# Score matmuls of the first key tile placed ahead of the sums of the second one in a stick-breaking attention

## The chip, the core and the metric

The kernel runs on one core of a Trainium2 chip. The metric is device time in microseconds (us) of one execution; the median of three runs of the kernel before is 2151.57 us (2151.13 to 2152.0). Engines are named as in the profile: PE is TensorE's matmul and PEld its weight load, DVE is VectorE, ACT is ScalarE, POOL is GpSimd, SP is SyncE, which issues DMAs.

## What is computed

Two layers over 528 tokens (16 meta tokens and 512 frames) of width 1024. Each layer is a half SwiGLU, a mixer and a half SwiGLU. The mixer projects the normed input, runs a stick-breaking attention beside a convolution branch, gates and adds both and projects again. The attention is the part that matters here:

```python
def block(args):                       # for one block of queries, 8 heads of 64
    qb, start = args
    z = jnp.einsum('bhqd,bhkd->bhqk', qb, kh) * scale
    qpos = start + jnp.arange(Q_BLOCK, dtype=jnp.int32)[:, None]
    valid = key_pos < qpos
    log_keep = jnp.where(valid, jax.nn.log_sigmoid(-z), 0.0)
    after = lax.cumsum(log_keep, axis=3, reverse=True) - log_keep
    attn = jnp.where(valid, jnp.exp(jax.nn.log_sigmoid(z) + after), 0.0)
    return jnp.einsum('bhqk,bhkd->bhqd', attn, vh)
```

So the weight of a key needs the sums over all later keys up to the query. Key tiles are therefore worked from the last one (3) down to the first one (0).

## The kernel before

Everything is kept transposed: channels on the 128 partitions, tokens along the row. Each float32 matrix is split in a high and a low float32r part (`split`, L79 and L80: a cast on ACT, a subtraction on DVE), and each product is three matmuls (high·high, high·low, low·high). The weights of a projection come by DMA in units of 1024x128, are split by ACT (L224, L225) with a DMA that adds on POOL's queue (L226), and are prepared three units ahead (`LOOK`).

In the mixer, `attend(i, ...)` (called four times a layer, each time for a pair of heads) and `products()` (the projections q, k, v, gs and gc) are two generators that take turns. After each `yield` of `attend`, `next(beside)` issues one piece of a projection: 24 matmuls of 264 columns, or 12 of 512, at L720, into a PSUM tile `ps`, which DVE reads out at L795. The projections have nothing to do with the attention of the same pair; they are there to keep PE busy while ACT and DVE work on the scores. PE's order is exactly the order of the calls (`manual_schedule` at L987). On ACT, DVE, POOL and SP the scheduler sets the order.

For one pair, `attend` works in these steps. The opening transposes v (L836, L840) and multiplies the corner pieces (L845) into a PSUM tile `zt`. `scores(t)` multiplies q by k for key tile t (L877, six matmuls) and adds the mask (L880) into a PSUM tile `z`; then `softplus` goes over it: the absolute value (L814), Exp and Ln (L103) on ACT, a maximum and an addition on DVE (L817); then the split in `sh` and `sl`. `sums_and_weights(t)` adds the running sums onto the same `z` by matmuls with a matrix of ones and a triangle (L900, L902, L903), lets POOL fold `sl` into the next tile's (L906), and takes Exp of `z` on ACT (L913, recorded as L103, output `a`), which is split in `ah` and `al`. `values(t)` multiplies them by v (L921). The last three steps of a pair, `sums_and_weights(0)`, `values(1)` and `values(0)`, are run by `step` inside the next pair's `attend`, or after the last pair between the remaining projections.

The score tiles are five a pair, and the pool that holds them has two buffers, used in turn:

```python
tc.tile_pool(name=f"psz{l}", bufs=2, space=bass.MemoryType.PSUM, reuse_waits="tile") as psz:
...
    return psz.tile([P, 2, 512], F32, tag="z", name="z")
```

In the order zt, t=3, t=2, t=1, t=0 the tile of t=0 takes the buffer of t=2, and the next pair's `zt` takes the buffer of t=1. A tile's buffer is free for the next when all that read it are done; the last reader of a score tile is the Exp at L913.

The rest of this section prints the code with the profile's line numbers.

Of the kernel before, what the change touches and what calls it, by code (L numbers as in the profile page):

```python
# [60 lines left out]
def kernel(ctx, tc, hT, par, const, wg1, wu1, wd1, win, wao, wco, wout, wg2, wu2, wd2, out):  # L61
# [12 lines left out]
    def f(ap):  # L74
        return ap.bitcast(F32)

    def split(x, hi, lo):

        act.copy(hi, x)  # L79
        dve.tensor_tensor(out=lo, in0=x, in1=f(hi), op=ALU.subtract)  # L80
# [15 lines left out]
    def fn(out, in_, func, **kw):  # L96
        need = SETS[func]
        if table["set"] != need:
            load = act.preload_act_table_set(need)
            for p in table["acts"]:  # L100
                tc.add_manual_dep(load.ins, p.ins.name, NOSYNC, reason="table order")
            table.update(set=need, load=load, acts=[])
        i = act.activation(out, in_, func, **kw)  # L103
        tc.add_manual_dep(i.ins, table["load"].ins.name, NOSYNC, reason="table order")
        table["acts"].append(i)
# [570 lines left out]
    PIECES = ((3, 272, 256, 0), (2, 256, 272, 112), (1, 128, 400, 112), (0, 16, 512, 128))  # L676

    def mixer(l, st, omode, after):
        last = omode == XO
        with ExitStack() as es:  # L680
# [72 lines left out]
            with tc.tile_pool(name=f"psm{l}", bufs=2, space=bass.MemoryType.PSUM, reuse_waits="tile") as psp, \  # L753
                    tc.tile_pool(name=f"psz{l}", bufs=2, space=bass.MemoryType.PSUM, reuse_waits="tile") as psz:

                def ztile():
                    return psz.tile([P, 2, 512], F32, tag="z", name="z")
# [28 lines left out]
                with tc.tile_pool(name=f"att{l}", bufs=1, reuse_waits="tile") as ap_:  # L786
# [26 lines left out]
                    def softplus(dst, z, np_):  # L813
                        act.activation(dst, z, AF.Abs)  # L814
                        fn(dst, dst, AF.Exp, bias=bias[:np_, 3:4], scale=-1.0)
                        fn(dst, dst, AF.Ln, bias=bias[:np_, 2:3], scale=1.0)
                        dve.scalar_tensor_tensor(out=dst, in0=z, scalar=0.0, in1=dst, op0=ALU.max, op1=ALU.add)  # L817
# [6 lines left out]
                    def attend(i, step, qf, kf, vf):  # L824
# [45 lines left out]
                        def scores(t, q0, n, m0):  # L870
                            z = ztile()
                            ks = slice(t * P, (t + 1) * P)

                            for pi, (kk, qq) in enumerate(((kh, qh), (kh, ql), (kl, qh))):
                                for hh in range(2):
                                    r = slice(64 * hh, 64 * hh + 64)
                                    pe.matmul(z[:, hh, :n], kk[r, ks], qq[r, q0:q0 + n], start=(pi == 0), stop=False,  # L877
                                              skip_group_check=True)
                            for hh in range(2):
                                pe.matmul(z[:, hh, DEAD[t]:240 - m0], identb, maskb[:, m0 + DEAD[t]:], start=False, stop=False,  # L880
                                          skip_group_check=True)
                            d = DEAD[t]
                            sp = ap_.tile([P, 2, 512], F32, tag="big", bufs=BIG, name="sp")[:, :, d:n]
                            sh, sl = rests if t == 3 else (ap_.tile([P, 2, n], F32R, tag=f"s{x}{t}" if t else "big",
                                                                    bufs=1 if t else BIG, name=f"s{x}") for x in "hl")
                            softplus(sp, z[:, :, d:n], P)
                            if t == 3:
                                dve.tensor_tensor(out=sp[96:128, :, n - d - 16:], in0=sp[96:128, :, n - d - 16:],
                                                  in1=corner[96:128], op=ALU.subtract)
                            split(sp, sh[:, :, d:], sl[:, :, d:])  # L890
                            later[t] = (z, sh, sl, q0, n)

                        def sums_and_weights(t):
                            z, sh, sl, q0, n = later[t]
                            for hh in range(2):

                                for e in range(3, t, -1):
                                    _, ph, pl, pq, pn = later[e]
                                    for s in (ph, pl) if e == t + 1 else (ph,):
                                        pe.matmul(z[:, hh, pq - q0:pq - q0 + pn], onesm, s[:, hh, :], start=False,  # L900
                                                  stop=False, skip_group_check=True)
                                pe.matmul(z[:, hh, :n], trir, sh[:, hh, :], start=False, stop=False, skip_group_check=True)  # L902
                                pe.matmul(z[:, hh, :n], trir, sl[:, hh, :], start=False, stop=True, skip_group_check=True)  # L903
                            if 0 < t < 3:
                                _, _, pl, pq, _ = later[t + 1]
                                pool.tensor_tensor(out=sl[:, :, pq - q0:], in0=f(sl[:, :, pq - q0:]), in1=f(pl), op=ALU.add)  # L906
                            d = DEAD[t]
                            a = ap_.tile([P, 2, 512], F32, tag="big", bufs=BIG, name="a")[:, :, d:n]
                            ah, al = (ap_.tile([P, 2, 512], F32R, tag="big", bufs=BIG, name=nm)[:, :, :n]
                                      for nm in ("ah", "al"))  # L910
                            for p in (ah, al) if d else ():
                                pool.memset(f(p[:, :, :d]), 0.0)
                            fn(a, z[:, :, d:n], AF.Exp, bias=B_ZERO)  # L913
                            split(a, ah[:, :, d:], al[:, :, d:])
                            acts[t] = (ah, al, q0, n)
# [35 lines left out]
                        values(3)  # L951
                        sums_and_weights(2)
                        yield
                        sums_and_weights(1)
                        scores(*PIECES[3])
                        yield
                        values(2)
                        yield
# [28 lines left out]
                    with tc.manual_schedule(engines={mybir.EngineType.PE}):  # L987
                        for i in range(4):
                            for _ in attend(i, step, *parts(i)):
                                next(beside, None)  # L990
                        for n, fill in enumerate(FILL_END):
                            for _ in range(fill):
                                next(beside, None)
                            step(n)
                        for _ in beside:
                            pass
# [152 lines left out]
```

## Time and profile before

| What | us |
|---|---|
| median of three runs | 2151.57 |
| time of the profiled execution | 2152.29 |
| its span, first to last instruction | 2150.5 |
| PE busy in the span | 2135.9 (99%) |
| PEld busy | 2052.8 (95%) |
| DVE busy | 1521.5 (71%) |
| ACT busy | 1137.9 (53%) |
| POOL busy | 488.7 (23%) |

The granted clock of TensorE is 0.999 of full speed over the span. Busy shares are averages over the whole program; matmuls are pipelined, so their rows overlap, and what a matmul takes is read from the distance between the starts of two that follow each other. The attention of layer 0 lies at about 436 to 617 us, that of layer 1 at about 1512 to 1686 us. A boundary between two pairs is the opening (L836) of the next pair; there are three a layer.

### The profile page before, as it was taken

Reading aid. Unit: us, or ns where it says so; the run is one execution under the profiler, and the core shown is the slowest. Engines: PE = TensorE matmul, PEld = TensorE weight load, DVE = VectorE, ACT = ScalarE, POOL = GpSimd, SP = SyncE. Lnnn points to the kernel's source line nnn. Section 1 sums busy time; section 2 is a strip of 40 time slices with the busy share of each in tenths; the row PEclk is TensorE's granted clock in tenths of the full one; section 3 lists DMA queues with packets and bytes.
Section 4 is the critical chain, followed back from the end, with each engine's and each line's share of the span. In section 5 each row is a group of like instructions: output and inputs, shape, how many; then the busy total and the mean of one; then the engine's idle time right before and its main releaser. Section 6 shows DMA issues by size and latency. Waiting matters only on the chain.

```text
span 2150.5 us, 39932 instructions
## 1 busy us (share of the span) xinstructions
PE 2135.9 (99%) x16226; PEld 2052.8 (95%) x16226; DVE 1521.5 (71%) x2091; ACT 1137.9 (53%) x1587; POOL 488.7 (23%) x449
## 2 busy tenths in 40 slices
PE   9999999999999999999999999999999999999998
PEld 9999999999999999999999999999888889999897
DVE  7867685677766777677877676856677767767685
ACT  6434355467776545343554443554778775444354
POOL 1322321211111131313113223212112111322320
PEclk9999999999999999999999999999999999999999
DMA  8465536865578747464365655368656886665542
GB/s 236 133 165 141 142 104 198 181 138 119 134 169 180 175 129 189 129 161 122 99 169 145 168 140 146 103 193 184 142 127 133 187 188 167 159 175 143 144 111 77
DMA packets 140168, 324.90 MB, mean 151 GB/s; under 512 B 15568, under 2 KB 19664, under 8 KB 139984
## 3 DMA queue, kind: packets, MB, share of 16 engines
q1 hardware_dynamic: 101856, 226.36, 33.3%
q0 software_dynamic: 37440, 95.44, 26.1%
q8 instruction: 127, 2.08, 0.4%
q10 hardware_dynamic: 688, 0.55, 0.1%
q14 instruction: 57, 0.47, 0.1%
HBM read 315.86 MB, written 6.42 MB: 150 GB/s over the span
## 4 chain that ended last, share of the span: by engine, by line
PE 99%; ACT 0%; DVE 0%; DMA 0%; issue 0%; DVEq 0%; ACTq 0%
PE pb L580 16%; PE ps L580 16%; PE ps L720 15%; PE ps L260 12%; PE ps L706 10%; PE pe L260 6%; PE pb L260 6%; PE pe L580 5%; PE z L706 2%; PE ps L502 2%; PE pe L502 1%; PE pb L502 1%; PE z L877 1%; PE po L921 1%; PE z L900 1%; PE ps L554 1%
## 5 line engine op out<-in xcount | busy, mean ns | idle before, releaser
L79 ACT CAST wh<-wr 128x1024 fp32r<-128x1024 f32 (+4 forms) x275 | 242.2, 887 | 372.4 <-PE ps L260 94.5
L80 DVE TENSOR_TENSOR wl<-wr,wh 128x1024 fp32r<-128x1024 f32 (+4 forms) x275 | 300.6, 1096 | 57.4 <-ACT wh L79 53.5
L79 ACT CAST wh<-s 128x1024 fp32r<-128x1024 f32 x158 | 165.8, 1049 | 274.9 <-DVE s L236 83.1
L80 DVE TENSOR_TENSOR wl<-s,wh 128x1024 fp32r<-128x1024 f32 x158 | 216.1, 1368 | 59.4 <-ACT wh L79 58.7
L720 PE MATMUL ps<-uh,wh 128*128 128x264 f32 (+1 forms) x792 | 243.8, 308 | 0.0
L720 PE MATMUL ps<-uh,wl 128*128 128x264 f32 (+1 forms) x792 | 240.0, 303 | 0.0
L720 PE MATMUL ps<-ul,wh 128*128 128x264 f32 (+1 forms) x792 | 239.9, 303 | 0.0
L640 POOL TENSOR_TENSOR h<-h,dt 128x528 f32<-128x528 f32 (+1 forms) x96 | 179.9, 1879 | 258.1 <-DVE dt L638 255.2
L210 POOL DMA_DIRECT2D s<-wg x78 | 72.8, 938 | 596.9 <-DMA s<-wg 337.9
L748 DVE SCALAR_TENSOR_TENSOR y<-uc,prm,y 128x528 f32<-128x528 f32 (+1 forms) x240 | 197.7, 824 | 4.1
L224 ACT CAST wh<-wr 128x1024 fp32r<-128x1024 f32 x104 | 109.1, 1049 | 141.2 <-issue 46.9
L580 PE MATMUL ps<-ul,wh 128*128 128x264 f32 (+1 forms) x624 | 177.4, 284 | 0.0
L580 PE MATMUL pb<-sl,wh 128*128 128x264 f32 (+1 forms) x624 | 176.9, 283 | 0.0
L580 PE MATMUL ps<-uh,wl 128*128 128x264 f32 (+1 forms) x624 | 176.9, 283 | 0.0
L580 PE MATMUL pb<-sh,wl 128*128 128x264 f32 (+1 forms) x624 | 176.8, 283 | 0.0
L580 PE MATMUL pb<-sh,wh 128*128 128x264 f32 (+1 forms) x624 | 176.5, 283 | 0.0
L580 PE MATMUL ps<-uh,wh 128*128 128x264 f32 (+1 forms) x624 | 176.2, 282 | 0.0
L720 PEld LDWEIGHTS ps<-uh,wl 128*128 128x128 f32 x792 | 149.1, 188 | 5.9
L720 PEld LDWEIGHTS ps<-uh,wh 128*128 128x128 f32 x792 | 148.9, 188 | 5.4
L720 PEld LDWEIGHTS ps<-ul,wh 128*128 128x128 f32 x792 | 149.0, 188 | 5.1
L260 PE MATMUL ps<-ah,wh 128*128 128x264 f32 (+1 forms) x616 | 142.0, 300 | 0.0
L260 PE MATMUL ps<-ah,wl 128*128 128x264 f32 (+1 forms) x616 | 141.8, 300 | 0.0
(319 smaller groups left out, 6460.8 us busy)
## 6 DMA issues: line engine op xcount, KB each, us to landing
wr<-wd SPq DMA_DIRECT2D x96, 384.0 KB, 3.6
wr<-win SPq DMA_DIRECT2D x72, 512.0 KB, 4.4
wl<-win POOLq DMA_DIRECT2D x72, 512.0 KB, 7.8
wr<-wg SPq DMA_DIRECT2D x117, 256.0 KB, 3.0
wr<-wu SPq DMA_DIRECT2D x117, 256.0 KB, 3.4
s<-wg SPq DMA_DIRECT2D x78, 256.0 KB, 5.2
s<-wu SPq DMA_DIRECT2D x78, 256.0 KB, 5.7
s<-wg POOLq DMA_DIRECT2D x78, 256.0 KB, 5.2
```

The costliest lines, as they stand in the source:

```text
L79: act.copy(hi, x)
L80: dve.tensor_tensor(out=lo, in0=x, in1=f(hi), op=ALU.subtract)
L210: pool.dma_start(t[:, a:b], src, accum_op=ALU.add)
L224: act.copy(hi[:, :nk], raw[:, :nk])
L260: pe.matmul(ps[:, c, :n], wt[:, k0 + k, :], xt[:, s:s + n], start=(k == 0 and pi == 0), stop=(k == end and pi == 2))
L502: pe.matmul(ps[:, e, :TH], wt[:, k, :], xt[:, s], start=(k == ORDER[0] and pi == 0), stop=(k == ORDER[-1] and pi == 2))
L554: pe.matmul(ps[:, e, :TH], wt[:, k, :], xt[:, s], start=(k == 0 and pi == 0), stop=(k == KD - 1 and pi == 2))
L580: pe.matmul(ps[:, e, :TH], wt[:, 4 * e + kk, :], xt, start=start and kk == 0 and pi == 0, stop=kk == 3 and pi == 2, skip_group_check=True)
L640: pool.tensor_tensor(out=tri(h[j], mode), in0=tri(h[j], mode), in1=tri(t, mode), op=ALU.add)
L706: pe.matmul(ps, wt[:, k0 + k, :], xt[:, s], start=(n == 0 and pi == 0), stop=(n == nk - 1 and pi == 2))
L720: pe.matmul(ps, wt[:, k, :], xt[:, s], start=(n == 0 and pi == 0), stop=(n == KD - 1 and pi == 2))
L748: t = dve.scalar_tensor_tensor(out=y, in0=uc[i][:, c0 + k:k + T], scalar=col(w0 + k), in1=y, op0=ALU.mult, op1=ALU.add)
```

## The change

In `attend`, two calls that stand in one step, between the same two `yield`s, change places: the scores of key tile 0 are issued before the sums of key tile 1. Nothing is added or removed.

```diff
                         values(3)
                         sums_and_weights(2)
                         yield
+                        scores(*PIECES[3])
                         sums_and_weights(1)
-                        scores(*PIECES[3])
                         yield
                         values(2)
                         yield
```

The scheduler's order on the other engines follows from it. On PE, in the first pair of layer 0, the order after the last matmul of a projection piece (numbers tell the tiles apart; z_5536 is key tile 1, the z that L877 writes is key tile 0; the second head's sums, which repeat the first's, are left out) is this before:

```order
L720 MATMUL ps_5609<-uh7_4482,wl_5251 128x264
L900 MATMUL z_5536<-sh_5050,onesm_116 128x256
L900 MATMUL z_5536<-sh_5449,onesm_116 128x272
L900 MATMUL z_5536<-sl_5450,onesm_116 128x272
L902 MATMUL z_5536<-sh_5546,trir_118 128x400
L903 MATMUL z_5536<-sl_5547,trir_118 128x400
L877 MATMUL z_5654<-qh_5285,kh_5287 128x512 x2
L877 MATMUL z_5654<-ql_5286,kh_5287 128x512 x2
L877 MATMUL z_5654<-qh_5285,kl_5288 128x512 x2
L880 MATMUL z_5654<-maskb_120,identb_119 128x112
L720 MATMUL ps_5680<-uh0_4165,wh_5371 128x264
```

And this in the change:

```order
L720 MATMUL ps_5609<-uh7_4482,wl_5251 128x264
L877 MATMUL z_5637<-qh_5285,kh_5287 128x512 x2
L877 MATMUL z_5637<-ql_5286,kh_5287 128x512 x2
L877 MATMUL z_5637<-qh_5285,kl_5288 128x512 x2
L880 MATMUL z_5637<-maskb_120,identb_119 128x112
L900 MATMUL z_5536<-sh_5050,onesm_116 128x256
L900 MATMUL z_5536<-sh_5449,onesm_116 128x272
L900 MATMUL z_5536<-sl_5450,onesm_116 128x272
L902 MATMUL z_5536<-sh_5546,trir_118 128x400
L903 MATMUL z_5536<-sl_5547,trir_118 128x400
L720 MATMUL ps_5680<-uh0_4165,wh_5371 128x264
```

The eight score and mask matmuls moved ahead of the ten sums; what stands before and behind both is the same.

On ACT, at the same place (a<-z of 128x2x400 is the Exp of key tile 1, sp of 128x1024 the softplus of key tile 0, kh and qh are the splits for the next pair), the order before is:

```order
L225 ACTIVATE wl<-wr 128x1024
L103 ACTIVATE a<-z,bias 128x2x400
L79 CAST kh<-k 128x512
L79 CAST ah<-a 128x2x400
L79 CAST qh<-q 128x528
L814 ACTIVATE sp<-z 128x1024
L103 ACTIVATE sp<-sp,bias 128x1024 x2
L79 CAST sh<-sp 128x1024
L224 CAST wh<-wr 128x1024
```

And in the change:

```order
L225 ACTIVATE wl<-wr 128x1024
L814 ACTIVATE sp<-z 128x1024
L79 CAST kh<-k 128x512
L103 ACTIVATE sp<-sp,bias 128x1024
L79 CAST qh<-q 128x528
L103 ACTIVATE sp<-sp,bias 128x1024
L79 CAST sh<-sp 128x1024
L103 ACTIVATE a<-z,bias 128x2x400
L224 CAST wh<-wr 128x1024
L79 CAST ah<-a 128x2x400
```

The Exp of key tile 1 went from the first place behind wl to the place behind sh, past the whole softplus of key tile 0. The same rows stand at all six boundaries between pairs (in layer 1 with q of 128x512).

On DVE, at the same place, the order before is:

```order
L80 TENSOR_TENSOR kl<-k,kh 128x512
L80 TENSOR_TENSOR al<-a,ah 128x2x400
L80 TENSOR_TENSOR ql<-q,qh 128x528
L795 SCALAR_TENSOR_TENSOR gs<-ps,rstd 128x264
L748 SCALAR_TENSOR_TENSOR y_5183<-uc_4720,prm,y_5183 128x528 x2
L817 SCALAR_TENSOR_TENSOR sp<-z,sp 128x1024
```

And in the change:

```order
L80 TENSOR_TENSOR kl<-k,kh 128x512
L80 TENSOR_TENSOR ql<-q,qh 128x528
L795 SCALAR_TENSOR_TENSOR gs<-ps,rstd 128x264
L817 SCALAR_TENSOR_TENSOR sp<-z,sp 128x1024
L748 SCALAR_TENSOR_TENSOR y_5183<-uc_4720,prm,y_5183 128x528 x2
L80 TENSOR_TENSOR sl<-sp,sh 128x1024
```

The maximum-and-add of key tile 0 (sp) now stands right behind the read-out gs, ahead of two steps of the convolution (L748), and al of key tile 1 has gone behind sl.

## Rows read from the trace of the kernel before

**Rows 1.** The profile's page, busy time: engine, us, share, instructions.
```profile
PE 2135.9 (99%) x16226; PEld 2052.8 (95%) x16226; DVE 1521.5 (71%) x2091; ACT 1137.9 (53%) x1587; POOL 488.7 (23%) x449
```
**Rows 2.** Waits of PE: line, waited for, total us, times, longest; the whole list.
```profile
PE ps L554 <- ACT wh L79: 4.8, 1, 4.8
PE z L924 <- ACT vb L862: 0.2, 1, 0.2
```
**Rows 3.** PE in time, layer 0, first pair: start, length, line, tiles.
```profile
463.39 0.40 PE L900 MATMUL z<-sh,onesm 128*128 128x256 f32 x2
...
463.93 0.43 PE L903 MATMUL z<-sl,trir 128*128 128x400 f32 x1
...
464.74 0.34 PE L903 MATMUL z<-sl,trir 128*128 128x400 f32 x1
465.01 0.50 PE L877 MATMUL z<-qh,kh 64*128 64x512 f32 x2
...
465.91 0.27 PE L880 MATMUL z<-maskb,identb 128*128 128x112 bf16 x2
...
472.42 0.27 PE L836 MATMUL z<-cc,v 128*16 128x128 f32 x1
```
**Rows 4.** Weight loads (PEld) in time, same place.
```profile
463.92 0.19 PEld L903 LDWEIGHTS z<-sl,trir 128*128 128x128 f32 x1
```
**Rows 5.** ACT in time, same place; in brackets idle time before.
```profile
460.65 0.72 ACT L103 ACTIVATE a<-z,bias 128x544 f32<-128x544 f32 x1 [1.20 <-PE z L903]
...
464.42 1.06 ACT L225 ACTIVATE wl<-wr 128x1024 fp32r<-128x1024 f32 x1
465.38 0.91 ACT L103 ACTIVATE a<-z,bias 128x800 f32<-128x800 f32 x1
466.19 0.61 ACT L79 CAST kh<-k 128x512 fp32r<-128x512 f32 x1
...
467.46 0.63 ACT L79 CAST qh<-q 128x528 fp32r<-128x528 f32 x1
467.99 1.03 ACT L814 ACTIVATE sp<-z 128x1024 f32<-128x1024 f32 x1
469.05 2.34 ACT L103 ACTIVATE sp<-sp,bias 128x1024 f32<-128x1024 f32 x2
472.68 1.05 ACT L79 CAST sh<-sp 128x1024 fp32r<-128x1024 f32 x1 [1.29 <-DVE sp L817]
473.64 1.04 ACT L224 CAST wh<-wr 128x1024 fp32r<-128x1024 f32 x1
```
**Rows 6.** DVE in time, same place.
```profile
462.88 0.98 DVE L80 TENSOR_TENSOR sl<-sp,sh 128x800 fp32r<-128x800 f32 x1
...
464.76 2.54 DVE L748 SCALAR_TENSOR_TENSOR y<-uc,prm,y 128x528 f32<-128x528 f32 x2
...
468.73 0.69 DVE L80 TENSOR_TENSOR ql<-q,qh 128x528 fp32r<-128x528 f32 x1
469.35 0.42 DVE L795 SCALAR_TENSOR_TENSOR gs<-ps,rstd 128x264 f32<-128x264 f32 x1
469.69 1.56 DVE L748 SCALAR_TENSOR_TENSOR y<-uc,prm,y 128x528 f32<-128x528 f32 x2
471.43 1.22 DVE L817 SCALAR_TENSOR_TENSOR sp<-z,sp 128x1024 f32<-128x1024 f32 x1 [0.18 <-ACT sp L103]
```
**Rows 7.** POOL in time, same place.
```profile
465.22 1.51 POOL L906 TENSOR_TENSOR sl<-sl 128x544 fp32r<-128x544 f32 x1 [2.83 <-PE z L903]
```
**Rows 8.** PE in time, openings: layer 0 third boundary, layer 1 first.
```profile
558.54 0.27 PE L836 MATMUL z<-cc,v 128*16 128x128 f32 x1
...
1547.26 0.27 PE L836 MATMUL z<-cc,v 128*16 128x128 f32 x1
```
**Rows 9.** ACT in time, wl ahead of the same two openings.
```profile
550.54 1.05 ACT L225 ACTIVATE wl<-wr 128x1024 fp32r<-128x1024 f32 x1
...
1539.49 1.06 ACT L225 ACTIVATE wl<-wr 128x1024 fp32r<-128x1024 f32 x1
```

## The prediction

> **What bounds the kernel now.** I read the busy times first: PE is busy 99% of the span and no other engine is above 71% [rows 1]. Next the list of what PE waits for [rows 2]. It has two lines, 4.8 us at the start of a SwiGLU and 0.2 us at the first pair's corner piece, so 5.0 us of 2150.5 in all. Nothing in the attention holds PE up for a time worth having: a change of order there has next to nothing to win, and what it can do is make PE wait where it does not wait now. So I went to the step that the change touches and read PE, ACT and DVE in time side by side [rows 3, 5, 6], for the first pair of layer 0, and then the same place at other boundaries [rows 8, 9].
>
> What is to be seen there. PE does the sums of key tile 1 from 463.39 on, and the scores of key tile 0 from 465.01 to 465.91 + 0.27 = 466.18 [rows 3]. The next pair's opening (L836) is issued at 472.42 [rows 3]. It writes a score tile that takes over the buffer of key tile 1, so it has to come after the Exp of key tile 1. That Exp runs on ACT at 465.38 for 0.91 us and ends at 466.29 [rows 5]: PE comes 6.1 us later, and the buffer is long free. This margin is what the change spends.
>
> **The change, part by part.**
>
> PE's own work. Eight score and mask matmuls change places with ten sums in each pair; their number, columns and the pieces before and behind are the same. The step from a 128-row product to the 64-row scores is there once in either order (before it follows L903, then it will follow a projection's matmul). I take nothing for it; an estimate from the 465.01 - 464.74 = 0.27 us that this step takes now [rows 3] is that it can shift by 0.1 us at most either way, in eight places.
>
> A wait that goes. In the first pair the first L903 lasts 0.43 us, the second 0.34 [rows 3]. The first waits for `sl` of key tile 1, which DVE ends at 462.88 + 0.98 = 463.86 [rows 6]; its weight load starts at 463.92 [rows 4]. With the scores ahead this matmul comes about 1 us later and the 0.09 us are gone. Taken for the four pairs of layer 0: 4 x 0.09 = 0.36 us won. I count none for layer 1.
>
> A wait that is added ahead of the scores. Their tile takes the buffer of key tile 2, whose Exp ends at 460.65 + 0.72 = 461.37 [rows 5]. They now start at 463.39, so 2.0 us remain. Cost nothing; the cover would have to shrink by 2 us.
>
> A wait that is added at the opening, the term that decides. ACT now takes the softplus of key tile 0 first, and the Exp of key tile 1 behind `sh`. An ACT instruction starts 0.10 us before the end of the one ahead (wl 464.42 + 1.06, next 465.38 [rows 5]). The scores end at about 463.39 + 1.17 = 464.56, before ACT is done with wl, so the absolute value starts at 465.38. Then kh at 465.38 + 1.03 - 0.10 = 466.31, Exp at 466.31 + 0.61 - 0.10 = 466.82, qh at 466.82 + 1.17 - 0.10 = 467.89 (1.17 is half of the 2.34 of Exp and Ln), Ln at 467.89 + 0.63 - 0.10 = 468.42, ending at 469.59 [rows 5].
>
> DVE's maximum-and-add follows 0.04 us behind Ln (469.05 + 2.34 = 471.39, started 471.43), but behind the read-out gs, after which DVE was free for its next instruction at 469.69 [rows 6]; gs may come a little earlier now, since only kl and ql stand before it. I take 469.65. It ends 1.22 later at 470.87; `sh` starts 0.03 behind it, at 470.90; the Exp of key tile 1 starts 0.96 behind that (472.68 to 473.64), at 471.86, and ends 0.91 later, at 472.77 [rows 5, 6]. PE's weight load can then start 0.06 later and the matmul 0.01 behind it, as the waiting L903 shows [rows 3, 4, 6]: 472.84 against 472.42. PE waits **0.42 us**.
>
> From the start of wl to the opening that is 8.42 us. At the third boundary of layer 0: 550.54 + 8.42 = 558.96 against 558.54, again 0.42 [rows 8, 9]. At the first of layer 1 no read-out stands before the maximum, which makes it 8.40: 1539.49 + 8.40 = 1547.89 against 1547.26, so **0.63 us** [rows 8, 9]. There are three boundaries in each layer (the last pair of a layer has no opening behind it): 3 x 0.42 + 3 x 0.63 = 3.15 us lost.
>
> What queues behind. Behind the opening on PE stand the corner products; the chain of small ACT and DVE steps on them comes behind the same ACT work as before and is needed at the first L924 some 10 us on. The sums of key tile 0 get `sh` and `sl` earlier than now. On POOL the add of L906 goes behind one DMA of wl and starts about 1 us later; its result is wanted at the sums of key tile 0, nine us on. SP's loads of h move around one weight load behind the last pair, for weights needed tens of us later. All cost nothing under PE's projections.
>
> [...] The waiting L903 shows its weight load held back as well: load at 463.92, matmul at 463.93 [rows 3, 4]. [...]
>
> ACT stood idle for 1.29 us ahead of `sh`, with the cast wh behind it, which it did only after `sh` [rows 5]. [...]
>
> **Sum.** 3.15 - 0.36 = 2.8 us more. The profiled execution took 2152.29, 0.72 above the median; on it that gives 2155.1, on the median of the runs **2154.4 us**, 0.13% more. A difference under 0.2%, 4.3 us, is about what a measurement of this kernel cannot tell from none, so the forecast is "no change", on the slow side of it.
>
> **Bounds.** From below: no wait at all, and the L903 wait gone, 2151.57 - 0.36 = 2151.2. From above: each opening waits for one more convolution step on DVE beside POOL's add, 2.54 / 2 = 1.27 us [rows 6], 6 x 1.27 = 7.6 on top, 2162. I take the sum, since every step of it has its own row.
>
> **The rivals.**
> Forecast, 0.66: the openings wait 0.3 to 0.75 us each; 2153 to 2155.8.
> No wait, 0.16: ACT reaches the Exp in time, because the absolute value or a hand-over goes quicker than in my chain. For it: the wait of 0.42 is only 5% of a chain of 8.4 us. Against it: the chain starts at wl, which itself waits for PE, and no row has a shorter form of any link. Time: 2151.2. There is no path to faster by 0.2%, since PE has only 5.0 us of waits in the whole program and 4.8 of them lie elsewhere; I leave 0.02 for what I don't see.
> Slower, 0.16: POOL's add (1.51 us from 465.22 now [rows 7]) moves into kl and ql. A DVE step beside it takes 1.27 us, one without it 1.56 / 2 = 0.78 [rows 6]. If kl and ql are stretched by 0.5 us, gs and the maximum come 0.5 later, and each opening waits 0.9 to 1.1: 2.8 + 6 x 0.5 = 5.8, 2157.4. It decides from 0.25 us of delay per boundary on ((4.3 - 2.8) / 6). Against it: ql waits for qh anyway, until 468.5 in my chain, when the add should be over (1.51 us from about 466.2).
> That the change does not do what it says is excluded by the order shown.
>
> **The numbers.** 2154.4 is the forecast's middle. The range 2151.1 to 2156.8 takes in "no wait" and the beginning of "slower", leaving out under 2 in 10. Faster by over 0.2%: 0.02. Within: forecast, "no wait" and what lies between, 0.82. Slower: 0.16.
>
> **What would show it.** Right: PE's wait list has L836 with ACT's Exp (L103, tile a) as the releaser, six times, 0.3 to 0.75 us each, longer in layer 1; ACT's row of 128x800 Exp ends just before; PE's busy time hardly changes. Wrong: no such line; or L836 waiting over 0.8 us with the maximum (L817) starting late behind kl, ql or gs; or new waits of projections (L720) for weights or read-outs.

## The result and the profile after

The changed kernel takes 2154.91 us (median of 19 runs, 2154.03 to 2155.61); the kernel before, measured beside it, 2151.63 (19 runs, 2150.96 to 2152.32). The ratio is 1.0015 with a 95% interval of 1.0009 to 1.0021: 3.28 us slower, real, and within the 0.2% that was taken as no change. The forecast was 2154.4, between 2151.1 and 2156.8.

The profiled execution took 2154.51 us with a span of 2152.7 at a granted clock of 0.999. Its span is only 2.2 us longer than that before, because the stretch ahead of this place, in which the two kernels do the same, took 1.08 us less in this execution (the Exp of key tile 2 at 459.57 below, at 460.65 in [rows 5]). 2.2 + 1.08 = 3.28.

The page's first part, which answers to [rows 1]: no engine's work changed.

```profile
PE 2135.8 (99%) x16226; PEld 2052.0 (95%) x16226; DVE 1519.3 (71%) x2091; ACT 1136.6 (53%) x1587; POOL 490.4 (23%) x449
```

What PE waits for in the changed kernel, the whole list (line, releaser: total us, times, longest). Against [rows 2] there is one new line: the opening, L836, waits for ACT's Exp (L103, output `a`), six times.

```profile
PE ps L554 <- ACT wh L79: 4.7, 1, 4.7
PE z L836 <- ACT a L103: 2.5, 6, 0.5
PE z L924 <- ACT vb L862: 0.2, 1, 0.2
```

PE in time at the first pair of layer 0 and at four of the six openings (start, length, line, tiles, idle time before and its releaser), to be held against [rows 3, 8]:

```profile
462.40 0.50 PE L877 MATMUL z<-qh,kh 64*128 64x512 f32 x2
...
463.39 0.49 PE L900 MATMUL z<-sh,onesm 128*128 128x256 f32 x2
...
464.03 0.35 PE L903 MATMUL z<-sl,trir 128*128 128x400 f32 x1
...
464.77 0.34 PE L903 MATMUL z<-sl,trir 128*128 128x400 f32 x1
...
471.80 0.28 PE L836 MATMUL z<-cc,v 128*16 128x128 f32 x1 [0.34 <-ACT a L103]
...
558.83 0.28 PE L836 MATMUL z<-cc,v 128*16 128x128 f32 x1 [0.35 <-ACT a L103]
...
1548.19 0.28 PE L836 MATMUL z<-cc,v 128*16 128x128 f32 x1 [0.49 <-ACT a L103]
...
1632.68 0.28 PE L836 MATMUL z<-cc,v 128*16 128x128 f32 x1 [0.49 <-ACT a L103]
```

Two things are to be seen. The scores stand ahead of the sums, and the first L903 is now as short as the second (0.35 and 0.34 us, where the first had 0.43). And the openings wait. The idle time in brackets begins at the end that the profile models for the matmul before, and so it understates the loss: that matmul starts at 471.18 and is put at 0.28 us, but where nothing waits the opening starts 0.12 us behind the start of the matmul before it (472.30 and 472.42 in the kernel before). From start to start the first opening is 0.62 us behind, so it waits 0.50. The distance of the openings tells what a pair loses in all. Before it was (558.54 - 472.42) / 2 = 43.06 us a pair in layer 0 [rows 3, 8], and in layer 1 (1630.42 - 1547.26) / 2 = 41.58, with this last opening of the kernel before (PE in time):

```profile
1630.42 0.27 PE L836 MATMUL z<-cc,v 128*16 128x128 f32 x1
```

Now it is (558.83 - 471.80) / 2 = 43.515 and (1632.68 - 1548.19) / 2 = 42.245: **0.455 us more a pair in layer 0 and 0.665 in layer 1**. Three boundaries of each make 1.365 + 1.995 = 3.36 us, and 3.28 were measured.

ACT in time at the same place of the changed kernel, against [rows 5]: the Exp of key tile 1 (128x800, at 470.83) stands behind the whole softplus and `sh` of key tile 0, and ends at 470.83 + 0.92 = 471.75; the opening starts at 471.80.

```profile
459.57 0.72 ACT L103 ACTIVATE a<-z,bias 128x544 f32<-128x544 f32 x1 [1.19 <-PE z L903]
...
463.34 1.06 ACT L225 ACTIVATE wl<-wr 128x1024 fp32r<-128x1024 f32 x1
464.30 1.01 ACT L814 ACTIVATE sp<-z 128x1024 f32<-128x1024 f32 x1
465.21 0.60 ACT L79 CAST kh<-k 128x512 fp32r<-128x512 f32 x1
465.71 1.16 ACT L103 ACTIVATE sp<-sp,bias 128x1024 f32<-128x1024 f32 x1
466.77 0.62 ACT L79 CAST qh<-q 128x528 fp32r<-128x528 f32 x1
467.29 1.16 ACT L103 ACTIVATE sp<-sp,bias 128x1024 f32<-128x1024 f32 x1
469.87 1.05 ACT L79 CAST sh<-sp 128x1024 fp32r<-128x1024 f32 x1 [1.43 <-DVE sp L817]
470.83 0.92 ACT L103 ACTIVATE a<-z,bias 128x800 f32<-128x800 f32 x1
```

DVE and POOL in time there (one fence for each), against [rows 6, 7], and DVE's kl in the kernel before:

```profile
465.85 1.69 DVE L80 TENSOR_TENSOR kl<-k,kh 128x512 fp32r<-128x512 f32 x1 [0.60 <-ACT kh L79]
467.46 0.69 DVE L80 TENSOR_TENSOR ql<-q,qh 128x528 fp32r<-128x528 f32 x1
468.08 0.42 DVE L795 SCALAR_TENSOR_TENSOR gs<-ps,rstd 128x264 f32<-128x264 f32 x1
468.56 1.23 DVE L817 SCALAR_TENSOR_TENSOR sp<-z,sp 128x1024 f32<-128x1024 f32 x1
```
```profile
465.31 1.67 POOL L906 TENSOR_TENSOR sl<-sl 128x544 fp32r<-128x544 f32 x1
```
```profile
467.22 0.68 DVE L80 TENSOR_TENSOR kl<-k,kh 128x512 fp32r<-128x512 f32 x1
```

POOL's addition did move beside kl: 1.67 us from 465.31, with kl beside it at 1.69 us from 465.85, where kl took 0.68 in the kernel before. The maximum still starts only 468.56 - (467.29 + 1.16) = 0.11 us behind the end of Ln.

### The profile page after: what moved, and what is told of

The parts are those of the page before. It is cut to its first block, busy times and chain, and to the rows that moved or that the text cites. A ratio compares the mean times of both kernels' runs of the same rounds, so it can differ in the third digit from the quotient of the medians.

```text
span 2152.7 us, 39928 instructions
## 1 busy us (share of the span) xinstructions
PE 2135.8 (99%) x16226; PEld 2052.0 (95%) x16226; DVE 1519.3 (71%) x2091; ACT 1136.6 (53%) x1587; POOL 490.4 (23%) x449
## 4 chain that ended last, share of the span: by engine, by line
PE 96%; ACT 1%; DVE 1%; issue 1%; DMA 0%; DVEq 0%; ACTq 0%
PE pb L580 16%; PE ps L580 16%; PE ps L720 14%; PE ps L260 12%; PE ps L706 10%; PE pe L260 6%; PE pb L260 6%; PE pe L580 5%; PE z L706 2%; PE ps L502 2%; PE pe L502 1%; PE pb L502 1%; PE po L921 1%; PE z L877 1%; PE z L900 1%
## 5 line engine op out<-in xcount | busy, mean ns | idle before, releaser
L748 DVE SCALAR_TENSOR_TENSOR y<-uc,prm,y 128x528 f32<-128x528 f32 (+1 forms) x240 | 189.6, 790 | 4.3
L226 POOL DMA_DIRECT2D wl<-win x72 | 62.3, 865 | 360.1 <-ACT wl L225 240.8
```

What stands on the lines that cost most here:

```text
L226: pool.dma_start(lo[:, :nk], src[:, :nk].bitcast(F32R), accum_op=ALU.add)
L748: t = dve.scalar_tensor_tensor(out=y, in0=uc[i][:, c0 + k:k + T], scalar=col(w0 + k), in1=y, op0=ALU.mult, op1=ALU.add)
```

## The experiments

The theory: the whole cost is ACT's order. The Exp that frees a score buffer stands behind work that does not free it, and the opening waits for the buffer. The main rival: PE's new order costs by itself, through what it moves on POOL and DVE.

**PE's order changed, ACT's order put back.** `scores` and `sums_and_weights` issue their matmuls in the changed order; key tile 0's softplus is issued after the Exp, which its first instruction has to follow on ACT (an order without a semaphore, which the kernel uses elsewhere).

```diff
-                        scores(*PIECES[3])
-                        sums_and_weights(1)
+                        softplus_of_0 = scores(*PIECES[3])
+                        softplus_of_0(sums_and_weights(1))
```

> TensorE keeps the changed order (scores of key tile 0 ahead of the sums of key tile 1), but on ScalarE the Exp of key tile 1 is put ahead of the Abs of key tile 0 again (the order is now kh, qh, a, ah, Abs, Exp, Ln, wh, sh). Theory (the 3.3 us come from ScalarE's order alone, through the buffer of z that the next pair's opening needs): the wait of L836's matmul for ScalarE's a is gone at all six boundaries, and the time goes back to that of the kernel before or a few tenths below, 2151.0 to 2151.8. Rival 1 (TensorE's new order costs by itself, by what it does to POOL's addition and VectorE's kl): the time stays at 2154 to 2155.5 with no such wait in the list. Rival 2 (the new wait takes another place): the opening is on time, but the sums of key tile 0 wait for sh and sl, which stand behind wh now; they had about 2 us to spare in the kernel before and lose about 1 of it, so I expect no wait there.

Measured: 2151.17 us against 2151.45 for the kernel before, ratio 0.9999 (0.9989 to 1.0008). The whole list of PE's waits, ACT in time, and two openings on PE:

```profile
PE ps L556 <- ACT wh L79: 4.8, 1, 4.8
PE z L938 <- ACT vb L867: 0.2, 1, 0.2
```
```profile
465.83 0.92 ACT L104 ACTIVATE a<-z,bias 128x800 f32<-128x800 f32 x1
...
467.61 1.01 ACT L816 ACTIVATE sp<-z 128x1024 f32<-128x1024 f32 x1
```
```profile
471.76 0.27 PE L841 MATMUL z<-cc,v 128*16 128x128 f32 x1
...
557.75 0.27 PE L841 MATMUL z<-cc,v 128*16 128x128 f32 x1
```

With the Exp ahead of the absolute value the new wait is gone from the list, and the time is that of the kernel before. PE's new order by itself costs nothing that shows here. The distance of the openings is (557.75 - 471.76) / 2 = 42.995 us, 0.065 less than before: that is what the shorter L903 is worth in a pair of layer 0. In layer 1, where the first L903 was as short as the second already (0.34 and 0.35 us), the distance is (1629.61 - 1546.45) / 2 = 41.58, as before.

**PE's order as before, ACT's order changed.** The mirror image: the sums stay ahead of the scores, and the Exp of key tile 1 has to follow `sh` of key tile 0 on ACT.

```diff
-                        sums_and_weights(1)
-                        scores(*PIECES[3])
+                        weights_of_1 = sums_and_weights(1)
+                        weights_of_1(scores(*PIECES[3]))
```

> TensorE keeps the order of the kernel before (sums of key tile 1, then scores of key tile 0), but on ScalarE the Exp of key tile 1 is put behind the whole softplus of key tile 0 and its cast sh (and the scheduler puts the cast wh ahead of it too). Theory: from the start of wl to the opening the chain has the length that it has in the changed kernel, 8.46 us, and one cast wh more, about 0.95 us: 9.4 us after wl at 464.42 is 473.8, where the opening came at 472.42, so 1.4 us of wait at each boundary of layer 0 and 1.6 us in layer 1, 9 us in all: 2160.6 (2158.5 to 2162.5), with TensorE's order unchanged. Rival (the cost comes from TensorE's order): the time stays at 2151 to 2152.

Measured: 2169.63 us (2166.14 to 2171.31), ratio 1.0082 (1.0069 to 1.0096). The sign is the theory's, the size twice what I had given it. ACT in time and the first opening on PE:

```profile
463.91 1.05 ACT L227 ACTIVATE wl<-wr 128x1024 fp32r<-128x1024 f32 x1
465.28 0.62 ACT L79 CAST kh<-k 128x512 fp32r<-128x512 f32 x1 [0.31 <-PE z L882]
465.80 0.63 ACT L79 CAST qh<-q 128x528 fp32r<-128x528 f32 x1
466.34 1.02 ACT L816 ACTIVATE sp<-z 128x1024 f32<-128x1024 f32 x1
467.39 2.34 ACT L104 ACTIVATE sp<-sp,bias 128x1024 f32<-128x1024 f32 x2
...
473.06 0.92 ACT L104 ACTIVATE a<-z,bias 128x800 f32<-128x800 f32 x1
```
```profile
474.03 0.28 PE L841 MATMUL z<-cc,v 128*16 128x128 f32 x1 [1.93 <-ACT a L104]
```

From wl to the opening it is 474.03 - 463.91 = 10.1 us, not the 9.4 that I had worked out. I had taken it as indifferent where the casts kh and qh stand. In the changed kernel they stand between the steps of the softplus, and from wl to the end of Ln it is 468.45 - 463.34 = 5.1 us. Here they stand ahead of it, kh waits 0.31 us for the scores, and it is 467.39 + 2.34 - 463.91 = 5.8. The cast wh (0.95 us) stands ahead of the Exp as expected. So each opening lost 2.1 us in layer 0 and 2.3 to 2.4 in layer 1, about 13.4 in all. That still leaves 3 us or so of the profiled execution's 2168.07. They are at the third opening of layer 0 and of layer 1 (stretches of time: us, length, busy time of PE, PEld, DVE, ACT and POOL with the instructions, granted clock, DMA share, GB/s; the opening starts at 564.38):

```profile
564.00:566.00 2.00, 1.62 (x19) 1.39 (x20) 1.61 (x3) 2.00 (x4) 0.42 (x1) 1.00 0.00 0
566.00:568.00 2.00, 2.00 (x12) 2.00 (x12) 1.29 (x3) 1.35 (x5) 0.44 (x1) 0.53 0.83 244
568.00:570.00 2.00, 2.00 (x12) 2.00 (x12) 0.49 (x1) 0.62 (x4) 0.00 (x0) 0.61 0.82 121
570.00:572.00 2.00, 2.00 (x13) 1.86 (x12) 1.87 (x3) 0.00 (x0) 0.00 (x0) 1.00 0.68 133
```

Behind this wait the granted clock fell to half (0.50 in each whole us from 566.38 to 569.38) for some 3.4 us, and PE's matmuls of the projections followed each other every 0.22 us in place of 0.12. It fell at two of the six waits. By what is left that is about 1.6 us a fall; from the third opening of layer 0 to the first of layer 1 it is 1.56 us longer than before, and from the last opening to the end 1.3.

**The opening a piece later.** If the wait is only a matter of when PE comes, a later opening covers it. ACT's order stays that of the changed kernel.

```diff
+                        if i:
+                            yield
                         ncor = 1 if last else 2
...
-                        yield
+                        if not i:
+                            yield
                         step(0)
```

> The changed kernel, with one projection piece (24 matmuls, 2.9 us) between the scores of the pair before and the opening that stood behind the opening before; nothing else moves on TensorE, and the Exp of key tile 1 keeps its place behind the softplus of key tile 0. Theory: the wait of 0.5 to 0.65 us at the opening is covered by the 2.9 us, so the list has no wait of L836's matmul any more and the time is that of the kernel before, 2151.0 to 2152.0. Rival (the chain behind the opening, L924's corner and the values, had no room for a later start): a new wait of some tenths of a us at L924 or at the scores of key tile 3 takes its place, 2153 to 2155. Rival (it was not this wait): 2154.5 to 2155.5.

Measured: 2150.95 us, ratio 0.9998 (0.9989 to 1.0007). PE's list has the same two waits as in the first experiment. The Exp ends at 470.67 + 0.92 = 471.59 (ACT), the opening (PE) comes at 474.02 and does not wait:

```profile
470.67 0.92 ACT L103 ACTIVATE a<-z,bias 128x800 f32<-128x800 f32 x1
```
```profile
474.02 0.27 PE L838 MATMUL z<-cc,v 128*16 128x128 f32 x1
```

**The Exp in ACT's gap.** The smallest remedy: the Exp stands between Ln and `sh`, where ACT is idle for 1.43 us.

```diff
-                        scores(*PIECES[3])
-                        sums_and_weights(1)
+                        ln, split_of_0 = scores(*PIECES[3])
+                        weight, split_of_1 = sums_and_weights(1)
+                        behind(weight, ln)
+                        behind(split_of_0(), weight)
+                        split_of_1()
```

> The changed kernel with one move on ScalarE: the Exp of key tile 1 stands between the Ln of key tile 0's softplus and its cast sh, where ScalarE stands idle for 1.4 us behind VectorE's maximum. Theory: Exp ends near 469.4 in the first pair, sh starts at 469.9 as it does now, so the opening has 1.9 us to spare, nothing else is later, and all six waits go: 2150.9 to 2151.8. Rival 1 (TensorE's order costs by itself): 2154 to 2155.5. Rival 2 (the place in front of the softplus matters, not the one in front of sh): the wait at L836 stays, at over 0.3 us.

Measured: 2151.21 us, ratio 0.9998 (0.9989 to 1.0007), and no wait of the opening. ACT and DVE in time:

```profile
467.85 1.15 ACT L104 ACTIVATE sp<-sp,bias 128x1024 f32<-128x1024 f32 x1
468.90 0.91 ACT L104 ACTIVATE a<-z,bias 128x800 f32<-128x800 f32 x1
470.37 1.05 ACT L79 CAST sh<-sp 128x1024 fp32r<-128x1024 f32 x1 [0.56 <-DVE sp L819]
```
```profile
466.40 1.67 DVE L80 TENSOR_TENSOR kl<-k,kh 128x512 fp32r<-128x512 f32 x1 [0.62 <-ACT kh L79]
```

The Exp takes 0.9 of the idle 1.43 us and `sh` is no later behind Ln than in the changed kernel (470.37 - 467.85 = 2.52 us, there 469.87 - 467.29 = 2.58). kl takes 1.67 us here too, where it took 0.68 in the kernel before, and the time is that of the kernel before: a longer kl by itself costs nothing that shows. In the changed kernel the maximum behind kl is on the way to the opening; there it starts 0.11 us behind Ln, where [rows 5, 6] have 0.04, so the longer kl can have added 0.07 us a boundary at most.

**Larger doses.** To see whether a us of wait costs a us, the chain was made longer in the changed kernel, first with a part of key tile 0's absolute value done twice, then with the Exp of key tile 1 done four times over (the same values each time).

```diff
+                            if t == 0:
+                                act.activation(sp[:, 0, :256], z[:, 0, d:d + 256], AF.Abs)
                             softplus(sp, z[:, :, d:n], P)
```
```diff
-                            fn(a, z[:, :, d:n], AF.Exp, bias=B_ZERO)
+                            for _ in range(4 if t == 1 else 1):
+                                fn(a, z[:, :, d:n], AF.Exp, bias=B_ZERO)
```

> The changed kernel with 256 of the 1024 columns of key tile 0's Abs done twice (about 0.3 us of ScalarE, as the 128x288 one takes 0.39); the scheduler then also puts the cast wh (0.95 us a step) ahead of the Exp of key tile 1. So the chain to the opening is 1.25 us longer: waits of 1.75 us in layer 0 and 1.9 in layer 1. Theory A (a us of wait costs a us and nothing else): 2154.9 + 6 x 1.25 = 2162.4. Theory B (a long wait of TensorE also takes the granted clock down behind it, as the run with waits of 2.1 to 2.3 us showed at two of six boundaries, 1.6 us each): each boundary at which the clock falls adds 1.6 us, up to 2172; the rows of the granted clock behind each opening say at which.

Measured: 2161.44 us, ratio 1.0046 (1.0033 to 1.0059). Two openings (PE), one of each layer:

```profile
564.15 0.28 PE L836 MATMUL z<-cc,v 128*16 128x128 f32 x1 [1.84 <-ACT a L103]
...
1596.61 0.28 PE L836 MATMUL z<-cc,v 128*16 128x128 f32 x1 [0.90 <-ACT a L103]
```

The openings stand 2.0 us a pair further apart than in the first experiment in layer 0, and 1.1 in layer 1, where the dose came out smaller than I had expected because the cast wh stayed behind the Exp there (ACT: the Exp at 1552.97, wh at 1553.79): 9.3 us in all, on 2151.2 that gives 2160.5. In the profiled execution (2161.09 us) the granted clock stayed at 1.00 behind all six openings. This is theory A, with the dose mis-sized in layer 1. It need not hold for every execution: two of the five, at 2161.68 and 2163.91 us, had a granted clock of 0.997 over the span, and none of the 42 executions of the kernel before beside these experiments was under 0.998. A fall or two of the clock would fit the slower one, 2.8 us above the profiled execution; neither has a trace.

> The changed kernel with the Exp of key tile 1 done four times over (0.82 us each; the scheduler puts wh and wl, 0.95 us each, between them), so the chain to the opening is 3 x 0.82 + 2 x 0.95 = 4.4 us longer and each wait 4.9 to 5.0 us. Theory A (a us of wait costs a us): 2154.9 + 6 x 4.4 = 2181. Theory B (the granted clock falls behind a long wait): it falls at all six boundaries here, and each fall costs about 1.6 us, 2190 to 2191.

Measured: 2193.73 us, ratio 1.0195 (1.0181 to 1.0209). The stretches around the second opening of layer 0 (at 526.18, columns as above):

```profile
524.00:526.00 2.00, 0.00 (x0) 0.00 (x0) 0.12 (x1) 1.97 (x3) 0.67 (x1) 0.77 0.34 61
526.00:528.00 2.00, 1.82 (x15) 1.42 (x16) 0.95 (x1) 1.17 (x3) 0.22 (x1) 0.50 0.74 221
528.00:530.00 2.00, 2.00 (x10) 2.00 (x10) 0.64 (x3) 1.24 (x4) 0.00 (x0) 0.50 0.95 182
530.00:532.00 2.00, 2.00 (x12) 2.00 (x11) 0.28 (x1) 0.61 (x4) 0.00 (x0) 0.53 0.32 64
```

Waits of 5.0 us and a little more, and the clock falls at every one of the six, here still inside the wait. 2193.7 - 2151.2 = 42.5 us; the waits are 30 of them, so the six falls cost 2.1 us each on average, more than the 1.6 that I took from the second experiment. They were longer: the clock stayed at half for 6.8 us at four of the six (at this one from about 525.1 to 531.9) and for 3.4 us at two. By the distances of the openings, less the waits, the two short ones cost 1.4 us each, as in the second experiment, and the four long ones 2.1 to 2.9. Theory B holds for waits of this length.

**The change in layer 1 alone.**

```diff
+                        if last:
+                            scores(*PIECES[3])
                         sums_and_weights(1)
-                        scores(*PIECES[3])
+                        if not last:
+                            scores(*PIECES[3])
```

> The change made in layer 1 alone; layer 0 keeps the order of the kernel before. Theory (the cost is a sum over the boundaries, 0.46 us each in layer 0 and 0.65 in layer 1, and nothing is handed on from layer to layer): three waits of L836's matmul for a left, all behind 1500 us, 1.5 to 2 us in all, and a time of 2153.2 to 2153.8. Rival (a later attention of layer 0 moves a transfer of weights that costs something too, or is needed for it): nearer to 2151.5, or to 2155.

Measured: 2153.51 us against 2151.73, ratio 1.0008 (0.9999 to 1.0017). The interval alone does not exclude "no change"; the list of PE's waits has the new line three times, and the openings of layer 0 are at 43.06 to 43.08 us from each other, as before the change:

```profile
PE z L836 <- ACT a L103: 1.5, 3, 0.5
```

So the cost is a sum over boundaries; nothing that shows is handed on from one layer to the other. No variant is measurably faster than the kernel before: the three that lose the wait came out at 2150.95 to 2151.21 against 2151.45, each with 1.0 inside its interval.

## Why the prediction was right

**PE's own work, nothing.** Right. The first and the third experiment keep PE's new order and have the time of the kernel before, and in layer 1 the openings of the first experiment are as far apart as before.

**A wait that goes, 0.36 us won.** This is the step that was wrong in its size, by an error in the counting. The wait at L903 does go, and is worth 0.065 us a pair (42.995 against 43.06), not 0.09. But in three of the four pairs of layer 0 it is won ahead of an opening that then waits for ACT, whose chain starts at wl, ahead of these sums: what PE gains there it waits longer at the opening. From start to start the third opening of layer 0 waits 0.64 - 0.12 = 0.52 us (558.83, the matmul before it at 558.19), and the pair loses 0.455. Only the last pair of the layer, behind which no opening stands, keeps it. The term is 0.07 us, not 0.36.

**A wait added ahead of the scores, nothing.** Right: PE's list has no line for L877.

**The opening's wait, the term that decides.** Right in place, releaser, number and size. The chain from wl to the opening was put at 8.42 us and measured 471.80 - 463.34 = 8.46. The differences are small: the steps from wl to the end of Ln took 5.11 us where I had 5.17, the maximum came 0.11 us behind Ln in place of 0.06, and the cast `sh` 0.05 later behind the maximum than I had it. In layer 1 it is 8.42 (wl at 1539.77, opening at 1548.19) for 8.40. Against the openings before, that makes 0.455 us a boundary in layer 0 and 0.665 in layer 1 where I had 0.42 and 0.63.

**The sum.** By the measured sizes 3 x 0.455 + 3 x 0.665 - 0.07 = 3.3 us. I had 2.8, and 3.28 were measured. Of the missing 0.5 us, 0.29 is the gain that was counted four times, and the rest 0.035 us at each of the six boundaries. One premise beside the sum did not hold: that a difference under 0.2% can hardly be told from none. This one is 0.15%, and its interval reaches 0.06% to either side.

**What queues behind, nothing.** Right: with the wait taken away by a later opening or an earlier Exp, nothing is left of the 3.3 us.

**The weight load, held back with its matmul.** Right, as the row of the waiting L903 had it. The weight loads (PEld) of the changed kernel at the first opening, and the one of the kernel before:

```profile
471.79 0.09 PEld L836 LDWEIGHTS z<-cc,v 128*16 128x16 f32 x1 [0.55 <-ACT a L103]
```
```profile
472.31 0.09 PEld L836 LDWEIGHTS z<-cc,v 128*16 128x16 f32 x1
```

Where nothing waited the load ran 0.11 us ahead of its matmul (472.31, 472.42). Where the pair waited, the load was held back with the matmul (471.79, 471.80), 0.04 and 0.05 us behind the end of the Exp at 471.75, so it shortened nothing at this wait.

The Exp did not slip into ACT's gap either: ACT idled 1.43 us ahead of `sh` with the Exp behind it, whose sums PE had ended at 464.77 + 0.34 = 465.1, and the fourth experiment had to put the Exp ahead by hand.

**"No wait"** did not come. **"Slower"** came by half: POOL's addition moved beside kl, and kl took 1.69 us there (0.68 in the kernel before), where the larger ql, behind the addition, took 0.69, as that rival has it. But what it was said to cost, 0.5 us, was hidden for the reason given against it: ql has to wait for qh anyway. The maximum started 468.56 - 463.34 = 5.22 us behind wl, where I had 469.65 - 464.42 = 5.23. It was a near thing: kl ended at 465.85 + 1.69 = 467.54 and qh at 466.77 + 0.62 = 467.39, so in layer 0 a still longer kl would have come through to the opening.

## What to carry to other kernels

When two steps change places on an engine that never waits, look at what order the other engines take them in: here the two steps on PE are free in either order, and the cost is that ScalarE then does the step that frees a buffer behind one that does not. Work that hands a buffer back belongs ahead of work that only fills the next one, or into a gap in which the engine waits for another; here the gap was free (2151.21 us, with the Exp's 0.9 us in the idle 1.43). And a gain upstream of a wait is not a gain: count it only where nothing downstream waits for a chain that started earlier.

## What the runs showed of the hardware

Some waits of TensorE cost more than their length here: 30 us of waits came to 42.5 us in the run with the longest. In the profiled executions the granted clock stayed at 1.00 behind waits of 0.5 to 0.7 us (six of six, changed kernel) and of 1.1 and 2.0 us (six of six). It fell to 0.50 at two of six waits of 2.1 to 2.4 us, and at six of six of 5.0 to 5.1 us. In the second experiment PE ran without a pause up to the wait ahead of 564.38 (busy 2.00 of the 2.00 us from 560 to 562), and behind it it did the opening's small matmuls before the next projection piece (564.38 to 565.34), with the clock falling at about 566.1. A fall of 3.4 us cost 1.3 to 1.6 us, one of 6.8 us 2.1 to 2.9. Why it fell at two of the six like waits and not at the others is not settled here. The four executions of that kernel, 2166.14, 2168.07, 2171.18 and 2171.31 us, had granted clocks of 0.998, 0.997, 0.996 and 0.996 over the span, which would fit one fall fewer and two more than the two that the trace of the second shows. So how many of such waits bring a fall differs from one execution to the next, as far as times and clocks without a trace can tell.

DVE's subtraction of 128x512 (kl) took 1.69 to 1.75 us at the six boundaries of the changed kernel, where POOL's addition (1.46 to 1.68 us) ran beside it, and 0.68 at the six of the kernel before, where the addition had ended 0.5 to 1.3 us ahead of it.
